# The upward products of both MLPs by seven half-size block products instead of eight

## The chip, the cores and the metric

The kernel runs on one core of a Trainium2 chip. The core has a matrix engine (PE in the profile), a vector engine (DVE), a scalar engine (ACT), a general engine (POOL) and a queue engine (SP) that issues most of the transfers (DMAs) between the chip's memory and the on-chip memory. The metric is the device time of one execution in microseconds (us); a smaller number is better.

## The reference, cut to what matters

The program is one inference step of a two-layer trunk: a Mamba-2 mixer, an MLP, an HGRN2 mixer, a second MLP and a last norm, over 512 prompt tokens and 32 sample tokens with 1024 features, all in float32. The changed part is the MLP, which stands twice:

```python
def rmsnorm(x, w):
    xf = x.astype(jnp.float32)
    y = xf * lax.rsqrt(jnp.mean(xf * xf, axis=-1, keepdims=True) + EPS)
    return (y * w.astype(jnp.float32)).astype(x.dtype)

def squared_relu_mlp(u, w_up, w_down):          # w_up (1024, 4096), w_down (4096, 1024)
    return jnp.square(jax.nn.relu(u @ w_up)) @ w_down

h = h + squared_relu_mlp(rmsnorm(h, norm_mlp_w[layer]), mlp_w_up[layer], mlp_w_down[layer])
```

## The kernel before

Features lie on the 128 partitions and the 544 tokens along the free axis, so a tile is 128 features by 544 tokens. `x` is kept as eight such tiles. A weight "unit" is 128 by 1024 words: for one tile of output features, eight blocks of 128 by 128, one for each tile of input features.

A float32 product is made of three products in a shorter format. Weight and operand are each split into a high part (`hi`, `uh`, `gh`), made by a cast on ACT, and the rest (`lo`, `ul`, `gl`), made by a subtraction on DVE; `split` does both. `products` then issues, for each of the k blocks and each half of the tokens (272 columns), hi by hi, hi by low and low by hi, so a unit takes 8 times 3 times 2 = 48 matmuls.

The weights arrive in the order of their use. `load_unit` issues one DMA of 512 KB into one of three buffers `raw`; `conv_unit` splits it into one of two pairs `whi`, `wlo`; `unit(u)` sees to it that unit u+1 is converted when unit u is used.

`mlp` runs in two halves of the 4096 inner features. In each half it makes 16 tiles of the inner layer: `up` makes the product in two banks of the accumulation memory (`pm`), DVE takes it out with relu and the factor 1/rms (`a`), ACT squares it, and `split` makes `gh`, `gl`. Then come the eight tiles of the output (`pd`), each over 16 inner tiles with two units, and `add_to_x` on DVE adds each to `x`. The accumulators `acc_tile` have two buffers of two banks; `mx` has four buffers of one bank.

The first `up` products run on the operand `uops`, that is x times the norm's weight and split, without 1/rms, since this comes later. Work that can run beside the large products is written as a generator and given to `background`; `tick` in `products` advances it by a step now and then, and `drain` runs what is left. The order in which instructions stand in each engine's queue is set by a scheduler from the program's text. `tc.high_priority()` lets the weight splits and the emptying of accumulators go ahead. Each engine runs its queue strictly in that order.

At the end of the second MLP `finish` makes the last output tile, one half of the tokens after the other, with the final norm and the output behind each.

Of the kernel before, what the change touches and what calls it, by code (L numbers as in the profile page):

```python
# [9 lines left out]
F32 = mybir.dt.float32  # L10
# [31 lines left out]
# ticks between the steps of what runs behind the large products: of the four groups of the first mixer, and of  # L42
# the pair weights and the states of the second
# [11 lines left out]
# columns of the small per-feature vectors, 128 features to a column  # L55
# [11 lines left out]
def trunk(ctx: ExitStack, tc: tile.TileContext, io):  # L67
# [31 lines left out]
    # the array's clock rises after some microseconds of work: products of zeros while the first loads are on the way  # L99
# [5 lines left out]
    ready = {}  # L105
    loaded = dict(enumerate(first))
    state = {"load": 2, "conv": 0}

    def load_unit():
        u = state["load"]  # L110
        if u >= N_UNITS:
            return
        state["load"] += 1
        raw = wraw.tile([P, 1024], F32, tag="raw", name=f"raw{u}")
        nc.sync.dma_start(raw, io["W"][u])
        loaded[u] = raw

    load_unit()
# [6 lines left out]
    def conv_unit():  # L125
        u = state["conv"]
        if u >= N_UNITS:
            return
        state["conv"] += 1
        with tc.high_priority() if u > 2 else ExitStack():  # L130
            while state["load"] <= min(u + 1, N_UNITS - 1):
                load_unit()
            raw = loaded.pop(u)
            hi = wcv.tile([P, 1024], F32R, tag="whi", name=f"whi{u}")
            lo = wcv.tile([P, 1024], F32R, tag="wlo", name=f"wlo{u}")
            for a in (0, 512) if u < 2 else (None,):
                c = slice(None) if a is None else slice(a, a + 512)
                split(raw[:, c], hi[:, c], lo[:, c], nc.gpsimd if 3 < u < U_MLP and u % 3 == 0 else None)
        ready[u] = (hi, lo)

    def unit(u):
        while state["conv"] <= min(u + 1, N_UNITS - 1):
            conv_unit()
        return ready.pop(u)
# [31 lines left out]
    def products(ps, hi, lo, ops, first, last):  # L176
        """ps[P, 2, HF] += w.T @ op over the k-tiles; hi, lo: (P, k, P); ops: k pairs of hi, lo."""
# [21 lines left out]
    def newton(ms, n):  # L199
        """ms ** -0.5 for ms > 0 of shape (p, n)."""  # L200
# [12 lines left out]
    def rstd_steps(scale, name, res, where, wait):  # L213
        """Along the free axis, the rows of 1 / rms of the tokens from their sums of squares in ssq."""
# [17 lines left out]
    def scaled_split(t, col, hi, lo):  # L232
        """hi + lo = t * col"""
# [11 lines left out]
    uh = [pers.tile([P, T], F32R, tag=f"uh{k}", name=f"uh{k}") for k in range(KT)]  # L245
    ul = [pers.tile([P, T], F32R, tag=f"ul{k}", name=f"ul{k}") for k in range(KT)]
    uops = list(zip(uh, ul))

    def pre_norm(v0):
        """For each tile of x: the operand x * w, split, and the sums of squares; 1 / rms multiplies the product."""  # L250
        def tile_done(k):
            scaled_split(x[k], vec[:, v0 + k : v0 + k + 1], uh[k], ul[k])
# [19 lines left out]
    # =====================================================================================  # L272
    def ssd(then):
# [24 lines left out]
        # x * w, split, and 1 / rms, which multiplies the products  # L298
# [25 lines left out]
        def conv_tile(u, ct, dst, rep):  # L324
            """One 128-feature tile of x, B, C: projection, causal convolution, silu."""
# [21 lines left out]
            # sample sequence s gives its four tokens at columns 515 + 7 s  # L347
# [26 lines left out]
        def silu2(u, zs, z):  # L374
            """zs = 2 silu(z)"""
# [4 lines left out]
        def first_gates():  # L380
            """The first four tiles of z: two side by side as x comes in; 1 / rms follows."""
# [26 lines left out]
        def normed():  # L408
            """The operand with 1 / rms in it."""
            for k in range(KT):  # L410
                t = pool.tile([P, T], F32, tag="st", bufs=4, name=f"xn{k}")
                if k % 3 == 1:
                    nc.gpsimd.tensor_tensor(t, x[k], rb, MUL)
                    scaled_split(t, vec[:, V_NMIX0 + k : V_NMIX0 + k + 1], uh[k], ul[k])
                else:
                    nc.vector.scalar_tensor_tensor(t, x[k], vec[:, V_NMIX0 + k : V_NMIX0 + k + 1], rb, MUL, MUL)
                    split(t, uh[k], ul[k])
# [4 lines left out]
        def scan(g, BT, CT, xs, par):  # L422
            """The recurrence of one group of 8 heads; its 4 tiles (two heads each) go to yr[g]."""
# [7 lines left out]
            def weights(c):  # L431
                """exp of the differences of the running sums, for 8 heads"""
# [7 lines left out]
            def tokens(c):  # L440
                """x * dt and x * dt * tail, tokens on partitions"""
# [13 lines left out]
            def inside(c):  # L455
                """The tokens of a chunk among themselves, and its part of the state"""
# [17 lines left out]
            def before(c):  # L474
                """What the tokens of a chunk take from the state before it"""
# [828 lines left out]
```

## Time and profile before

| | before |
|---|---|
| median of three runs | 1610.85 us (1610.6 to 1611.68) |
| span of the profiled execution, which is its own time in the trace | 1613.7 us |
| PE busy | 1572.6 us, 97% of the span |
| DVE busy | 966.1 us, 60% |
| ACT busy | 630.6 us, 39% |
| POOL busy | 145.4 us, 9% |
| granted clock of PE, mean over the span | 0.987 |
| first MLP, first `up` product to last `pd` product | 499.6 to 881.4 us |
| second MLP, the same, with its finish | 1211.4 to 1592.6 us |

The span is measured from the first to the last instruction of one profiled execution. The runs are executions of the same program without the profiler, 2.85 us below this span in the median. In the groups of the profile, a row gives line, engine, operation, output and inputs with their shapes, the count, the busy time in us and the mean duration of one in ns, then the idle time of the engine just before these instructions and what ended it. In the chain of waits a row gives start, duration and what ran.

### The profile page before, as it was taken

The numbers are of one execution on the slowest core, as the hardware profiler recorded it, in microseconds if no ns is written. First come the engines' busy times: TensorE is split into PE (matmuls) and PEld (weight loads), VectorE is DVE, ScalarE is ACT, GpSimd is POOL, SyncE is SP. The second block draws the span as 40 slices with busy tenths as digits, with TensorE's granted clock in tenths as the row PEclk, the third lists the DMA queues.
The fourth block names the chain that finished last, engine by engine and source line by source line (L and its number), as shares of the span: only waits on it lengthen the run. The fifth ranks groups of instructions, "written<-read, shape, count | busy, mean of one in ns | idle before, by whom it ended". The sixth has DMA issues, their size and how long they took to land.

```text
span 1613.7 us, 32119 instructions
## 1 busy us (share of the span) xinstructions
PE 1572.6 (97%) x13708; PEld 1515.9 (94%) x13708; DVE 966.1 (60%) x1654; ACT 630.6 (39%) x1135; POOL 145.4 (9%) x160
## 2 busy tenths in 40 slices
PE   8997989999999999999999999999999999999997
PEld 7896979989899999999999999999999999999997
DVE  7879787877876432244433688888875432244333
ACT  5485665756334431133332333333344331134321
POOL 4313131141310000000000000000000000000001
PEclk9998999999999999999999999999999999999998
DMA  5353444364232222232223222223222222322221
GB/s 182 109 156 103 160 120 157 101 197 120 88 103 85 87 92 89 82 92 92 90 89 118 70 93 91 85 91 111 81 93 80 92 81 90 92 85 86 92 92 56
DMA packets 74287, 164.38 MB, mean 102 GB/s; under 512 B 11105, under 2 KB 37761, under 8 KB 74145
## 3 DMA queue, kind: packets, MB, share of 16 engines
q1 hardware_dynamic: 72880, 161.19, 32.3%
q8 instruction: 108, 1.77, 0.5%
q10 hardware_dynamic: 1264, 1.14, 0.2%
q14 instruction: 35, 0.28, 0.1%
HBM read 145.13 MB, written 17.18 MB: 101 GB/s over the span
## 4 chain that ended last, share of the span: by engine, by line
PE 82%; DVE 5%; ACT 3%; DMA 2%; issue 2%; POOL 0%; SPq 0%; POOLq 0%; ACTq 0%; DVEq 0%
PE pm L182 24%; PE pd L182 23%; PE ps L182 18%; PE po L182 4%; PE pho L182 3%; DMA w<-cum_d 1%; PE pa L902 1%; PE py L468 1%; PE pu L459 1%; ACT w L436 1%; DVE wlo L123 1%; DVE ssq L243 1%; PE pi L484 1%; PE pn L603 1%; PE po L1028 0%
## 5 line engine op out<-in xcount | busy, mean ns | idle before, releaser
L122 ACT CAST whi<-raw 128x1024 fp32r<-128x1024 f32 (+1 forms) x226 | 235.3, 1041 | 686.1 <-PE pd L182 236.1
L123 DVE TENSOR_TENSOR wlo<-raw,whi 128x1024 fp32r<-128x1024 f32 (+1 forms) x209 | 259.7, 1242 | 164.2 <-ACT whi L122 153.0
L182 PE MATMUL ps<-uh,whi 128*128 128x272 f32 x1088 | 238.3, 300 | 1.6 <-ACT uh L122 0.8
L182 PE MATMUL ps<-ul,whi 128*128 128x272 f32 x1088 | 227.8, 291 | 0.5 <-DVE ul L123 0.5
L182 PE MATMUL ps<-uh,wlo 128*128 128x272 f32 x1088 | 228.2, 291 | 0.0
L182 PE MATMUL pm<-uh,whi 128*128 128x272 f32 x1024 | 212.0, 288 | 0.0
L182 PE MATMUL pm<-uh,wlo 128*128 128x272 f32 x1024 | 211.9, 288 | 0.0
L182 PE MATMUL pm<-ul,whi 128*128 128x272 f32 x1024 | 211.1, 288 | 0.0
L182 PE MATMUL pd<-gl,whi 128*128 128x272 f32 x992 | 204.8, 288 | 0.0
L182 PE MATMUL pd<-gh,whi 128*128 128x272 f32 x992 | 204.6, 288 | 0.0
L182 PE MATMUL pd<-gh,wlo 128*128 128x272 f32 x992 | 204.6, 288 | 0.0
L182 PEld LDWEIGHTS ps<-uh,whi 128*128 128x128 f32 x1088 | 172.8, 191 | 12.9 <-issue 6.5
L182 PEld LDWEIGHTS ps<-ul,whi 128*128 128x128 f32 x1088 | 173.5, 191 | 1.0 <-DVE ul L123 0.7
L182 PEld LDWEIGHTS ps<-uh,wlo 128*128 128x128 f32 x1088 | 172.7, 191 | 0.1
L797 DVE SCALAR_TENSOR_TENSOR a<-pm,m_rb 128x544 f32<-128x544 f32 x64 | 46.4, 725 | 195.6 <-PE pm L182 190.5
L182 PEld LDWEIGHTS pm<-uh,whi 128*128 128x128 f32 x1024 | 161.0, 188 | 0.0
L182 PEld LDWEIGHTS pm<-ul,whi 128*128 128x128 f32 x1024 | 160.9, 188 | 0.0
L182 PEld LDWEIGHTS pm<-uh,wlo 128*128 128x128 f32 x1024 | 159.9, 189 | 0.0
L182 PEld LDWEIGHTS pd<-gh,wlo 128*128 128x128 f32 x992 | 155.9, 188 | 0.0
L182 PEld LDWEIGHTS pd<-gh,whi 128*128 128x128 f32 x992 | 155.8, 188 | 0.0
L182 PEld LDWEIGHTS pd<-gl,whi 128*128 128x128 f32 x992 | 155.7, 188 | 0.0
L268 DVE TENSOR_TENSOR x<-pd,x 128x544 f32<-128x544 f32 x31 | 22.5, 725 | 122.0 <-PE pd L182 122.0
(354 smaller groups left out, 2236.2 us busy)
## 6 DMA issues: line engine op xcount, KB each, us to landing
raw<-in_W SPq DMA_DIRECT2D x222, 512.0 KB, 3.6
st<-in_ssm_in SPq DMA_DIRECT2D x16, 512.0 KB, 6.2
w<-cum_d SPq DMA_DIRECT2D x16, 512.0 KB, 5.5
out_ssm_s<-st SPq DMA_DIRECT2D x16, 512.0 KB, 3.7
hst<-in_hgrn_in SPq DMA_DIRECT2D x8, 512.0 KB, 4.3
out_hgrn_s<-hst SPq DMA_DIRECT2D x8, 512.0 KB, 4.4
E<-cum_d SPq DMA_DIRECT2D x24, 128.0 KB, 4.3
x<-in_xT SPq DMA_DIRECT2D x3, 544.0 KB, 6.7
```

Of the source, the lines that this page charges most:

```text
L122: nc.scalar.copy(hi, raw)
L123: (eng or nc.vector).tensor_tensor(lo, raw, hi.bitcast(F32), SUB)
L182: nc.tensor.matmul(ps[:, h, :HF], w[:, k, :], o[:, h * HF : (h + 1) * HF], start=(first and k == 0 and j == 0), stop=(last and k == n - 1 ...
L243: nc.vector.tensor_tensor(ssq[:, :T], ssq[:, :T], sq, ADD)
L268: nc.vector.tensor_tensor(v3(x[m]), ps[:, :, :HF], v3(x[m]), ADD)
L436: nc.scalar.activation(w[:, h], w[:, h], AF.Relu, bias=tok[:, 1, c, 8 * g + h : 8 * g + h + 1], scale=-1.0)
L459: nc.tensor.matmul(pu, bt[:, c], xts[c].rearrange("p h q -> p (h q)"), start=True, stop=True)
L468: nc.tensor.matmul(py[64 * (h % 2) : 64 * (h % 2) + 64, (h // 2) * P : (h // 2 + 1) * P], xds[c][:, h], ws_[c][:, h], start=True, stop=True,)
L484: nc.tensor.matmul(pi[:, j * P : (j + 1) * P], hT[:, j * P : (j + 1) * P], CT[:, cs], start=True, stop=True)
L603: nc.tensor.matmul(pn, bm[:, s], xq.rearrange("p h q -> p (h q)"), start=True, stop=True)
L797: nc.vector.scalar_tensor_tensor(v3(a), ps[:, :, :HF], 0.0, v3(res[0]), MAX, MUL)
L902: nc.tensor.matmul(pv4[b * NS : (b + 1) * NS, c], K[:, bs], QQ[:, 2 - n :, bs], start=True, stop=True, tile_position=(0, b * NS),)
```

## The change

Let the weights of two neighbouring tiles of inner features be a 2 by 2 arrangement of blocks: two tiles, each with its first four and its last four k blocks. The operand is cut alike: four and four tiles of input features, first and second half of the tokens. The product of the two is eight products of half size (12 matmuls each), and the change makes it from seven, by the scheme of Strassen in Winograd's form. The weight sums that it needs are made from the loaded weights, the operand sums once for each MLP, and the outputs are combined after the products.

- `MLP_GROUPS` is 4: the inner features are now in four groups of 8 tiles instead of two of 16. Each group's output products run over 8 inner tiles with one unit, so that each `x` tile is added to four times instead of twice for each MLP.
- The first group's eight tiles are made as before, 48 matmuls a tile. During its `pd` products `operands` makes the seven split operands (`b1`, two halves of `b2` and four halves of `t`) from the norm's operand. It adds high and low part on POOL, multiplies by 1/rms on DVE, and forms the sums; it does so in twelve steps, two ticks apart.
- The other three groups run in 4 pairs of tiles with the products `p1 p2 n6 q7 n5 p3 q4` (12 matmuls each, `seventh`); `SLOTS` interleaves the pairs, 7 slots a pair. `n6`, `n5` and `p3` go on in the bank of `p1`, and `q4` in that of `q7`; the values in between are copied out (`s1`, `sv`, `sw`, on ACT) and subtracted or added by DVE.
- For a pair, `load_next` loads the first tile's unit as `raw`, and three half units (`v` in two halves, and `a22`) for the second one. Then two DMAs that POOL issues add a half unit from memory onto `v` (`accum_op`). `form` makes the seven half-size weights: two sums `s2` on DVE and seven splits (`fh` on ACT, `fl` on DVE), with six buffers each. `v`, `a22` and `s2` have two buffers each.
- `_mlp_plan` writes the order out: the last output product of a group is cut in three pieces between the first products of the next, and the last two products of a group stand between pieces of the first two output products.
- `finish` now makes the last two output tiles, over 8 inner tiles each, in the same number of matmuls as before.

The function `g_tiles` squares a tile and splits it into `gh`, `gl` (ACT, ACT, DVE). The mixers' instructions stand as before on all engines.

```diff
+SLOTS = (("p1", 0), ("p2", 1), ("n6", 3), ("q7", 4), ("n5", 6), ("p3", 9), ("q4", 12))
+MLP_GROUPS = 4
+def _mlp_plan(ub):
+    plan = []
+    for q in range(MLP_GROUPS):
+        b = ub + 16 * q
+        if q == 0:
+            plan += [("u", b + i) for i in range(8)]
+        else:
+            slots = sorted((7 * i + t, name, b + 2 * i) for i in range(4) for name, t in SLOTS)
+            slots = [x[1:] for x in slots]
+            last = plan.pop()
+            piece = lambda k0, k1: last[:2] + (k0, k1) + last[4:]
+            plan += [piece(0, 4)] + slots[:2] + [piece(4, 6)] + slots[2:4] + [piece(6, 8)] + slots[4:]
+        downs = [("d", b + 8 + m, 0, 8, m, q) for m in range(KT)]
+        if q:
+            cut = lambda x, k0, k1: x[:2] + (k0, k1) + x[4:]
+            tail = plan[-2:]
+            plan[-2:] = [cut(downs[0], 0, 4), tail[0], cut(downs[0], 4, 6), tail[1], cut(downs[1], 0, 6), cut(downs[0], 6, 8), cut(downs[1], 6, 8)]
+            downs = downs[2:]
+        plan += downs
+    return plan
...
+    def load_next():
...
+            v = mp["w"].tile([P, 1024], F32, tag="v", bufs=2, name=f"v{u}")
+            a22 = mp["w"].tile([P, 512], F32, tag="a22", bufs=2, name=f"a22_{u}")
+            nc.sync.dma_start(v[:, :512], io["W"][u + 1][:, 512:])
+            nc.sync.dma_start(v[:, 512:], io["W"][u][:, :512])
+            nc.sync.dma_start(a22, io["W"][u + 1][:, 512:])
+            for c in (0, 512):
+                nc.gpsimd.dma_start(v[:, c : c + 512], io["W"][u + 1][:, :512], accum_op=ADD)
...
+    def form(name, u):
+        a1 = loaded["u", u]
+        v, a22 = loaded["v", u] if name not in ("p1", "p2") else (None, None)
+        if name == "n6":
+            s2 = mp["w"].tile([P, 512], F32, tag="s2", bufs=2, name=f"s2_{u}")
+            nc.vector.tensor_tensor(s2, v[:, 512:], a22, ADD)
+            loaded["s2", u] = s2
+        if name == "q7":
+            s2 = loaded["s2", u]
+            nc.vector.tensor_tensor(s2, s2, a1[:, 512:], ADD)
+        raw = {
+            "p1": lambda: a1[:, :512], "p2": lambda: a1[:, 512:], "n6": lambda: s2, "q7": lambda: v[:, 512:],
+            "n5": lambda: v[:, :512], "p3": lambda: loaded["s2", u], "q4": lambda: a22,
+        }[name]()
+        hi = mp["w"].tile([P, 512], F32R, tag="fh", bufs=6, name=f"fh{u}_{name}")
+        lo = mp["w"].tile([P, 512], F32R, tag="fl", bufs=6, name=f"fl{u}_{name}")
+        split(raw, hi, lo)
+        return hi, lo
...
+        def operands():
+            for k in range(4):
+                n = []
+                for j in (k, k + 4):
+                    t = pool.tile([P, T], F32, tag="a", name=f"{name}_n{j}")
+                    nc.gpsimd.tensor_tensor(t, uops[j][0].bitcast(F32), uops[j][1].bitcast(F32), ADD)
+                    nc.vector.tensor_tensor(t, t, res[0], MUL)
+                    n.append(t)
+                b11, b12, b21, b22 = n[0][:, :HF], n[0][:, HF:], n[1][:, :HF], n[1][:, HF:]
...
+                split(b11, *bo)
...
+                split(n[1], *bo)
...
+                yield 2
...
+                nc.vector.tensor_tensor(t1, b11, b12, SUB)
+                nc.vector.scalar_tensor_tensor(t2, t1, -1.0, b22, MUL, SUB)
+                nc.vector.tensor_tensor(t3, b12, b22, SUB)
+                nc.vector.tensor_tensor(t4, b21, t2, ADD)
+                yield 2
+                for i, (t, (n1, n2)) in enumerate(((t12, ("n5", "n6")), (t34, ("q7", "q4")))):
...
+                    split(t, *bo)
...
+                yield 2
...
+        def seventh(name_, u):
...
+            for k in range(4):
+                oh, ol = fops[name_, k]
+                for j, (w, o) in enumerate(((hi, oh), (hi, ol), (lo, oh))):
+                    nc.tensor.matmul(
+                        ps, w[:, k, :], o, start=(name_ in ("p1", "p2", "q7") and k == 0 and j == 0),
+                        stop=(k == 3 and j == 2), skip_group_check=name_ in ("n6", "n5", "p3", "q4"),
+                    )
+            tick()
+            keep = {"p1": "s1", "n6": "sv", "n5": "sw"}.get(name_)
+            with tc.high_priority():
+                if keep:
...
+                    nc.scalar.copy(d[keep], ps)
...
+                if name_ == "p2":
+                    nc.vector.tensor_tensor(d["p1"][:, :HF], ps, d["s1"], ADD)
+                if name_ == "n5":
+                    nc.vector.tensor_tensor(d["n6"][:, HF:], d["c"], d["sw"], SUB)
+                if name_ == "q4":
+                    nc.vector.tensor_tensor(d["n6"][:, :HF], ps, d["sv"], SUB)
+                if name_ == "p3":
+                    nc.scalar.activation(d["p1"][:, HF:], ps, AF.Relu)
+            if name_ == "p2":
+                nc.scalar.activation(d["p1"][:, :HF], d["p1"][:, :HF], AF.Relu)
+            if name_ == "p3":
+                g_tiles(u, d["p1"])
+            if name_ == "q4":
+                nc.scalar.activation(d["n6"], d["n6"], AF.Relu)
+                g_tiles(u + 1, d["n6"])
```

Two places in the queues matter below. The first is DVE during the first group of output products of the first MLP. Here `x` is the residual with the product `pd` added, `wlo` the low part of a weight unit, `m0_n` a norm's operand, `m0_b` and `m0_t` the sums' operands. Before, from the first addition on:

```order
L268 TENSOR_TENSOR x_75<-pd0_0_6624,x_75 128x544
L123 TENSOR_TENSOR wlo75_6738<-raw75_6679,whi75_6737 128x1024
L123 TENSOR_TENSOR wlo76_6792<-raw76_6735,whi76_6791 128x1024
L268 TENSOR_TENSOR x_75<-pd0_1_6734,x_75 128x544
L123 TENSOR_TENSOR wlo77_6848<-raw77_6789,whi77_6847 128x1024
```

Now, from the first addition to the second:

```order
L371 TENSOR_TENSOR x_75<-pd0_0_6147,x_75 128x544
L187 TENSOR_TENSOR wlo66_6227<-raw66_6148,whi66_6226 128x1024
L919 TENSOR_TENSOR m0_t34_0_6217<-m0_n4_6181,m0_t12_0_6216 128x272
L187 TENSOR_TENSOR m0_tl0_6255<-m0_t12_0_6216,m0_th0_6254 128x544
L187 TENSOR_TENSOR m0_b1l1_6293<-m0_n1_6286,m0_b1h1_6292 128x272
L187 TENSOR_TENSOR m0_tl4_6259<-m0_t34_0_6217,m0_th4_6258 128x544
L902 TENSOR_TENSOR m0_n5_6289<-m0_n5_6289,m0_rb_5734 128x544
L916 TENSOR_TENSOR m0_t12_1_6332<-m0_n1_6286 128x272
L918 TENSOR_TENSOR m0_t34_1_6333<-m0_n1_6286,m0_n5_6289 128x272
L917 SCALAR_TENSOR_TENSOR m0_t12_1_6332<-m0_t12_1_6332,m0_n5_6289 128x272
L187 TENSOR_TENSOR m0_b2l1_6297<-m0_n5_6289,m0_b2h1_6296 128x544
L371 TENSOR_TENSOR x_75<-pd0_1_6223,x_75 128x544
```

Before, an output product took two units, 96 matmuls, and DVE had two splits and one addition for it. Now it takes 48 matmuls, and DVE has one split, one addition and nine instructions of the operands.

The second place is the end of the second group of up products in the first MLP, where the fourth pair (units 78 and 79) ends. Before, DVE had for each tile the same three instructions:

```order
L797 SCALAR_TENSOR_TENSOR a70_6555<-pm70_6506,m0_rb_5715 128x544
L123 TENSOR_TENSOR wlo72_6565<-raw72_6500,whi72_6564 128x1024
L123 TENSOR_TENSOR gl70_6559<-a70_6555,gh70_6558 128x544
L797 SCALAR_TENSOR_TENSOR a71_6617<-pm71_6568,m0_rb_5715 128x544
L123 TENSOR_TENSOR wlo73_6628<-raw73_6562,whi73_6627 128x1024
```

Now, on DVE, with `s2_90` the sum of weights for the second pair of the next group:

```order
L187 TENSOR_TENSOR fl78_p3_7264<-s2_78_7112,fh78_p3_7263 128x512
L187 TENSOR_TENSOR fl78_q4_7268<-a22_78_7045,fh78_q4_7267 128x512
L187 TENSOR_TENSOR gl76_7191<-a76_p1_7003,gh76_7190 128x544
L216 TENSOR_TENSOR s2_90_7860<-v90_7772,a22_90_7773 128x512
L981 TENSOR_TENSOR a76_n6_7069<-pc76_7070,sv_76_7067 128x272
L979 TENSOR_TENSOR a78_n6_7214<-pc78_7215,sw_78_7259 128x272
L187 TENSOR_TENSOR gl77_7244<-a76_n6_7069,gh77_7243 128x544
```

And on ACT at the same place, where before a cast of `whi`, a square and a cast of `gh` came by turns (L122, L798, L122), now:

```order
L985 ACTIVATE a78_p1_7153<-a78_p1_7153 128x272
L938 ACTIVATE a76_p1_7003<-a76_p1_7003 128x544
L186 CAST gh76_7190<-a76_p1_7003 128x544
L973 COPY sv_78_7212<-pp78_7133 128x272
L989 ACTIVATE a76_n6_7069<-a76_n6_7069 128x544
L938 ACTIVATE a76_n6_7069<-a76_n6_7069 128x544
L973 COPY sw_78_7259<-pp78_7133 128x272
L186 CAST gh77_7243<-a76_n6_7069 128x544
```

The weight sum of the next group stands ahead of the emptying of the third pair's accumulator (`pc76`) on DVE. The relu of that result stands on ACT ahead of the copy `sw_78`, without which PE may not go on to the product `p3` of the fourth pair, in the same bank.

More of the change, by code (lines that the diff above doesn't have):

```diff
@@ L125, in conv_unit @@
     def conv_unit():
-        u = state["conv"]
-        if u >= N_UNITS:
+        if state["conv"] >= len(jobs):
             return
+        (kind, u), at = jobs[state["conv"]]
         state["conv"] += 1
         with tc.high_priority() if u > 2 else ExitStack():
[L131 to L138, printed above, removed]
@@ L139, in conv_unit @@
-        ready[u] = (hi, lo)
+            while state["load"] <= min(at + 1, len(loads) - 1):
+                if loads[state["load"]][0] == "v" and not mp:
+                    break
+                load_next()
+            if kind == "u":
+                raw = loaded.pop(("u", u))
+                hi = wcv.tile([P, 1024], F32R, tag="whi", name=f"whi{u}")
+                lo = wcv.tile([P, 1024], F32R, tag="wlo", name=f"wlo{u}")
+                for a in (0, 512) if u < 2 else (None,):
+                    c = slice(None) if a is None else slice(a, a + 512)
+                    split(raw[:, c], hi[:, c], lo[:, c], nc.gpsimd if 3 < u < U_MLP and u % 3 == 0 else None)
+            else:
+                hi, lo = form(kind, u)
@@ L141, in unit, with take @@
+    def take(key):
+        i = place[key]
+        ahead = 0.0
+        j = i
+        while j + 1 < len(jobs) and ahead < 1.0:
+            j += 1
+            ahead += 1.0 if jobs[j][0][0] == "u" else 0.25
+        while state["conv"] <= j:
+            if jobs[state["conv"]][0][0] != "u" and not mp:
+                break
+            conv_unit()
+        return ready.pop(key)
     def unit(u):
[L142 to L144 removed]
+        return take(("u", u))
```

202 lines of the change are left out of this document (135 added, 67 removed).

## The prediction

> **What bounds the kernel now.** I read the busy times first, then the chain of waits in the two MLPs, the busy times by stage, and the groups by shape of the MLP stages.
>
> ```profile
> PE 1572.6 (97%) x13708; PEld 1515.9 (94%) x13708; DVE 966.1 (60%) x1654; ACT 630.6 (39%) x1135; POOL 145.4 (9%) x160
> 505.29 87.27 PE pm L182 x696
> 592.56 96.19 PE pd L182 x768
> 688.75 96.22 PE pm L182 x768
> 784.98 96.37 PE pd L182 x768
> 1586.49 6.08 PE pd L1131 x48
> 688.00:785.00 97.00, 97.00 (x777) 97.00 (x776) 42.09 (x47) 36.06 (x47) 0.00 (x0) 1.00 0.28 88
> 592.00:688.00 96.00, 96.00 (x769) 96.00 (x768) 26.14 (x25) 18.06 (x18) 0.00 (x0) 1.00 0.28 89
> ```
>
> The chain of waits is PE alone in an MLP: 768 matmuls in 96.22 us are 125.3 ns each without a gap, at a granted clock of 1.00 (the third number from the end in a stage's row). The stages' rows give busy time of PE, weight loads, DVE, ACT and POOL. In an up stage DVE is busy for 42 of 97 us and ACT for 36; in an output stage 26 and 18 of 96. So fewer matmuls shorten the path one for one, as long as DVE and ACT, which get more to do, keep ahead. The row of L1131 has matmuls that go through one half of the tokens with another weight each time, as the new ones do: 6.08 / 48 = 126.7 ns. That the half-size products have a slower pace, so that the change doesn't do what it says, I therefore leave without a chance.
>
> **Removed from PE.** A pair of tiles takes 7 x 12 = 84 matmuls instead of 96. Twelve pairs in each MLP, two MLPs: 24 x 12 = 288 matmuls, at 125.3 ns 36.1 us. The output products and finish keep their count.
>
> **The prices of what is added.** All of it lies on DVE, ACT, POOL and the transfers. The nearest rows:
>
> ```profile
> L123 DVE TENSOR_TENSOR wlo<-raw,whi 128x1024 fp32r<-128x1024 f32 x16 | 19.6, 1225 | 1.7
> L937 DVE TENSOR_TENSOR att<-ac,bmask 128x512 f32<-128x512 f32 x8 | 5.5, 684 | 0.0
> L123 DVE TENSOR_TENSOR gl<-a,gh 128x544 fp32r<-128x544 f32 x15 | 10.9, 725 | 1.1
> L935 DVE TENSOR_TENSOR T<-f 128x272 f32<-128x272 f32 x8 | 3.5, 434 | 0.0
> L1135 DVE TENSOR_TENSOR x<-pd,x 128x272 f32<-128x272 f32 x2 | 0.9, 442 | 4.5 <-PE pd L1131 4.5
> L122 ACT CAST whi<-raw 128x1024 fp32r<-128x1024 f32 x17 | 17.8, 1049 | 64.9 <-PE pm L182 59.9 <-PE pd L182 5.0
> L122 ACT CAST whi<-raw 128x512 fp32r<-128x512 f32 x4 | 2.4, 612 | 2.2 <-DMA raw<-in_W 2.2
> L798 ACT ACTIVATE a<-a 128x544 f32<-128x544 f32 x15 | 9.9, 659 | 0.0
> L122 ACT CAST gh<-a 128x544 fp32r<-128x544 f32 x15 | 9.7, 648 | 0.5
> L334 ACT COPY pre<-ps 128x272 f32<-128x272 f32 x24 | 9.3, 388 | 0.0
> L1136 ACT ACTIVATE sq<-x 128x272 f32<-128x272 f32 x2 | 0.9, 431 | 8.1 <-DVE x L1135 8.1
> L313 POOL TENSOR_TENSOR sn_sq<-x 128x544 f32<-128x544 f32 x4 | 5.5, 1363 | 5.9 <-DMA x<-in_xT 5.9
> ```
>
> **The operands, during the first group's output products.** From the last inner tile's split to the weights of the eighth output product, DVE has 27 instructions of 544 (8 products with 1/rms, 4 low parts b2, 8 low parts t, 6 additions to x, one gl), 20 of 272, 7 weight splits and 6 instructions of 512: 27 x 0.725 + 20 x 0.434 + 7 x 1.225 + 6 x 0.684 = 41.0 us. PE needs the last of these weights after seven output products of 48 matmuls, 7 x 6.02 = 42.1 us. By that alone it fits, by one microsecond. But POOL adds high and low parts in the same stretch, six tiles of it at 1.36 us, 8.2 us, and the two engines shut each other out:
>
> ```profile
> 41.06 3.55 POOL L413 TENSOR_TENSOR xn<-x,sn_rb 128x544 f32<-128x544 f32 x1 [3.38 <-DVE ul L235]
> 42.05 1.34 DVE L123 TENSOR_TENSOR ul<-xn,uh 128x544 fp32r<-128x544 f32 x2
> 43.32 1.88 DVE L416 SCALAR_TENSOR_TENSOR xn<-x,vec,sn_rb 128x544 f32<-128x544 f32 x1
> 49.76 2.40 POOL L123 TENSOR_TENSOR wlo<-raw,whi 128x1024 fp32r<-128x1024 f32 x1 [3.12 <-ACT whi L122]
> 50.27 3.92 DVE L378 SCALAR_TENSOR_TENSOR zs<-thz,zs 128x544 f32<-128x544 f32 x3 [0.96 <-ACT thz L377]
> ```
>
> The POOL multiplication at 41.06 lasts 3.55 us, until two DVE instructions are through, and then the DVE instruction at 43.32 takes 1.88 us. Three DVE instructions of some 0.73 us that begin beside a POOL instruction at 50.27 take 3.92 us, 1.7 more. If all of it adds up, 41.0 + 8.2 - 42.1 = 7.1 us are lost in each MLP; if none, nothing. Two DVE instructions at 42.05 take 1.34 us together, less than twice 0.725, and the additions to x, which read the accumulators, may run beside POOL, so I take 3 us, nearer the lower end: 6 us for both MLPs (0 to 14). PE waits there for `wlo` of the fourth to eighth output product. [...]
>
> **The groups of pairs.** A pair now costs ACT seven casts of 512, three copies and two relus of 272, one relu, two squares and two gh of 544: 7 x 0.612 + 3 x 0.388 + 2 x 0.431 + 3 x 0.659 + 2 x 0.648 = 9.6 us. On DVE it is seven low parts and two sums of 512, three emptyings of 272 and two gl: 9 x 0.684 + 3 x 0.442 + 2 x 0.725 = 8.9 us. PE takes 84 x 0.1253 = 10.5 us for it. With the two weight units of the next output products that are split within a group of four pairs, add 0.5 us to ACT and 0.6 to DVE: 96% and 91% in the middle of a group. Over the whole group there is room, since the first pair's weights are made ahead, and an eighth output product and parts of two others lie around. In the middle the queues run late by an instruction or two. I followed three copies, behind which PE must wait to accumulate in the same bank: sv of the second pair comes about 0.5 us late (ACT waits before it for DVE, which waits for a22), sv of the fourth pair about as much, and sw of the fourth pair stands behind a chain that begins with a transfer. The two sv: 6 groups x 1.0 = 6 us (0 to 12, the upper end if each is late by a cast and a copy, 0.612 + 0.388 = 1 us).
>
> **The chain before sw.** The load of v for the next group's second pair needs the buffer that the fourth pair's n5 gives back when it is split. This split needs a buffer fl that is free after p1 of the fourth pair. From then to p3 of that pair PE has eight slots, 8 x 1.5 = 12.0 us. Within them: cast and split (0.612 + 0.684, plus some 2 us behind others in two full queues), the load, the added DMA, s2 (0.684), the emptying of q4 (0.442), relu and square (2 x 0.659), and sw (0.388). The loads:
>
> ```profile
> raw<-in_W SPq DMA_DIRECT2D x222, 512.0 KB, 3.6
> raw<-in_W SPq DMA_DIRECT2D x4, 256.0 KB, 5.4
> out_ssm_p<-hT SPq DMA_DIRECT2D x4, 256.0 KB, 2.0
> ```
>
> The load is 3.6 us. For the DMA that adds, which no row shows, the nearest are 2.0 and 5.4 us for 256 KB; I take 3.7. That makes 1.3 + 2 + 3.6 + 3.7 + 0.7 + 0.4 + 1.3 + 0.4 = 13.4 us against 12.0, 1.4 us late (none to 3.1). It happens twice in an MLP, for a third group has no next one: 4 x 1.4 = 5.6 us, 0 to 12.4. [...]
>
> **What costs nothing.** The 32 further additions to x (0.725 us) lie in output stages, where DVE has one split and one addition in 6 us. The bytes for a pair grow from 1 MB to 1.75 MB, in 10.5 us some 175 GB/s, twice the 88 to 89 of the stages' rows, with a DMA share of 0.28 there. Finish has the same matmuls, and its addition of squares runs beside the last tile's 24. If that cover were gone, it would cost two instructions, below 1 us.
>
> **The sum.** 36.1 - 6 - 6 - 5.6 = 18.5 us less: 1613.7 becomes 1595.2 us in the profiled execution, and 1610.85, the median of the runs, which lies 2.85 us below that span, becomes 1592.3.
>
> **Rivals.** *All hidden.* The queues keep ahead, since over a whole group ACT has 4 x 9.6 = 38 us to do while PE has 38 slots of 12 matmuls, 57 us (28 of the pairs, 4 of the eighth output product, 6 of two others), and the waits stay below 8 us: 1575 to 1583. [...]
>
> *ACT and DVE bound the groups.* If the new instructions take 10% longer than their nearest rows, ACT needs 10.6 + 0.5 us a pair against 10.5, and some 0.6 us is lost on three pairs of each of six groups, 11 us beyond the forecast; with the operands at their upper end another 8. That gives 1600 to 1608.
>
> *The added DMAs land late: slower.* POOL writes them out while DVE is 91% busy. If these DMAs take y us beyond 3.7, each of the four places before sw is later by y. In each of six groups the fourth pair's own s2 comes in too, once y passes some 6 us (its load goes out some nine slots before its use). Then 4y + 6(y - 6) is lost; 18.5 us are gone at y = 4.6, so it is slower from 8.3 us for an added DMA. At 10.5 us (y = 6.8) 32 us are lost: 1624. The row at 41.06 speaks for it: POOL waited 2 us there for DVE; against it, no transfer in the rows above took over 5.4 us. [...]
>
> **Chances.** The forecast (1583 to 1600) 0.44; all hidden 0.19; ACT and DVE as the bound 0.17; late DMAs 0.13, which is slower; the rest, 0.07, within 0.2% (3.2 us, about what a measurement of this kernel can tell from no change). So faster 0.80, same 0.07, slower 0.13. The range is 1575, where all is hidden, to 1612, which leaves out the late DMAs; the forecast's own range is 1583 to 1600.
>
> **What would show it.** Right: the up stages' chain of waits has 84 matmuls a pair at 125 ns; PE's idle time in an MLP is 6 to 12 us, in the first group's output products behind DVE `wlo`, and at the end of a group behind ACT `sw`. The first rival shows no such idle time, the second shows idle time before `fl` and `sv` in every pair, the third shows DVE `s2` waiting for the DMA `v`. I am wrong if PE's pace changes with the new products, or if an added DMA takes over 8 us.

## The result, and the profile after

The changed kernel took 1625.04 us in the median of four runs (1624.02 to 1626.94), the kernel before 1610.97 us beside it (1610.6 to 1611.68). The ratio is 1.0087, with a 95% interval of 1.0072 to 1.0101. The change made the kernel 14 us slower, where 18.5 us less were forecast.

The page's first rows show that the products did go away: PE has 288 matmuls less. But it is busy only 14 us less, not 36, and the span is longer, so PE must both wait and work more slowly:

```profile
span 1623.8 us, 32477 instructions
PE 1558.6 (96%) x13420; PEld 1489.0 (92%) x13420; DVE 1109.6 (68%) x1962; ACT 738.7 (45%) x1431; POOL 214.5 (13%) x224
```

From its first upward product (493.6 us before, 489.1 now) to the next mixer's first product the first MLP took 387.5 us before and takes 396.6 now; the second, to the end of its last output product, 390.0 and 394.4. (The table ahead of the change is short here: 499.6 is not the first upward product, and 1592.6 ends only the first half of the finish.) That is 13.5 us more together, near the 14.1 of the runs. With the 36.1 us that the removed matmuls were worth, about 50 us were lost in the two MLPs. The spans of the two profiles differ by only 10.1 us, because the profiled execution before came 4.5 us later to the first MLP. In the records of the runs a span lies 1.7 to 2.1 us below that run's own time, so the 2.85 us between the profile before and the median is a difference of executions.

The view of waits lists what PE waited for in the first MLP (us in total, times, longest); for the kernel before, the same view of that stretch is empty:

```profile
PE pm L282 <- DVE a L946: 3.9, 1, 3.9
PE pp L964 <- DVE a_p L977: 3.2, 2, 2.3
PE pp L964 <- ACT sw L973: 3.1, 5, 1.4
PE pd L282 <- DVE wlo L187: 2.1, 3, 1.8
PE pp L964 <- ACT s L973: 1.2, 3, 0.4
```

The first row is new to the forecast: an upward product `pm` of the *first* group, which the change left as it was, waits 3.9 us for the squared relu `a` on DVE. The chain of waits at that place (start, duration, what ran) leads from there to a transfer:

```profile
492.85 6.14 DMA v<-in_W
498.99 0.28 issue
499.27 7.03 DMA v<-in_W
506.31 0.02 issue
506.33 0.69 DVE s L216
507.02 0.65 DVE a L946
507.67 0.14 issue
507.80 4.25 PE pm L282 x20
```

L216 is `s2 = v + a22`, the first weight sum of a pair. DVE's timeline shows what it does there (in brackets the idle time before, and what ended it):

```profile
497.60 1.23 DVE L187 TENSOR_TENSOR wlo<-raw,whi 128x1024 fp32r<-128x1024 f32 x1 [0.27 <-ACT whi L186]
504.39 0.69 DVE L216 TENSOR_TENSOR s<-v,a 128x512 f32<-128x512 f32 x1 [5.56 <-DMA v<-in_W]
506.33 0.69 DVE L216 TENSOR_TENSOR s<-v,a 128x512 f32<-128x512 f32 x1 [1.25 <-DMA v<-in_W]
506.94 0.72 DVE L946 SCALAR_TENSOR_TENSOR a<-pm,m_rb 128x544 f32<-128x544 f32 x1
```

The two sums belong to pairs 72 and 74, which PE needs some 100 us later. The scheduler, to which they were given with high priority, put them in front of the squared relu that PE needs at once. DVE took them in that order, so it stood for 5.56 and 1.25 us before two loads while its next work, the squared relu, had been ready since 501.35, when ACT had copied its factor `m_rb`. What ended these waits were added DMAs, issued by POOL: the four at this place took 6.4 to 11.2 us from issue to landing. In the second MLP the first two sums stand in the same place and cost PE 3.1 us at 1233.68.

At the ends of the groups the chain before `sw` is the one that the forecast followed, with the transfers longer than it took them:

```profile
629.91 4.96 DMA a<-in_W
...
634.97 0.13 DVE s L216
...
635.58 0.45 DVE a_p L977
...
636.63 7.65 DMA v<-in_W
...
644.36 0.69 DVE s L216
645.05 0.36 DVE a_n L981
...
645.44 0.67 ACT a_n L989
...
646.13 0.66 ACT a_n L938
646.78 0.28 ACT sw L973
647.11 1.77 PE pp L964 x12
```

Here too `s2` stands on DVE in front of the emptying of a product (`a_p`, then `a_n`) and waits for `a22` and for `v`. DVE's own list of waits for the first MLP has these sums in two rows, the first with the two waits at the start in it:

```profile
DVE s L216 <- DMA v<-in_W: 17.6, 4, 5.9
DVE s L216 <- DMA a<-in_W: 8.3, 5, 2.9
```

The DMA issues give the medians from issue to landing:

```profile
v<-in_W SPq DMA_DIRECT2D x48, 256.0 KB, 4.4
v<-in_W POOLq DMA_DIRECT2D x48, 256.0 KB, 5.7
a<-in_W SPq DMA_DIRECT2D x24, 256.0 KB, 4.0
```

In the operand stage the rows by shape show DVE and POOL slowing each other. The low parts `b2l` and `b1l` were taken at 725 and 434 ns, the POOL addition at 1363:

```profile
L901 POOL TENSOR_TENSOR m_n<-uh,ul 128x544 f32<-128x544 f32 x6 | 10.1, 1677 | 27.3 <-DVE m_t L918 18.2 <-DVE m_t L919 5.9 <-ACT m_b1h L186 3.2
L902 DVE TENSOR_TENSOR m_n<-m_n,m_rb 128x544 f32<-128x544 f32 x8 | 6.9, 863 | 1.3 <-POOL m_n L901 1.3
L187 DVE TENSOR_TENSOR m_b2l<-m_n,m_b2h 128x544 fp32r<-128x544 f32 x4 | 4.9, 1215 | 0.0
L187 DVE TENSOR_TENSOR m_b1l<-m_n,m_b1h 128x272 fp32r<-128x272 f32 x4 | 4.1, 1023 | 0.0
```

And PE ran slowly for a while behind its stalls. In the chain above, 20 `pm` matmuls took 4.25 us instead of 2.5. The stages' rows (busy times of five engines, then granted clock, DMA share and GB/s) compare 3 us before that stall with 3 us behind it, behind the stall at `wlo` and behind the one at `a_p`:

```profile
500.00:503.00 3.00, 3.00 (x27) 3.00 (x26) 0.00 (x0) 0.67 (x2) 0.13 (x1) 1.00 1.08 264
508.00:511.00 3.00, 3.00 (x14) 3.00 (x15) 1.95 (x3) 2.49 (x4) 0.00 (x0) 0.50 0.00 0
572.00:575.00 3.00, 2.83 (x14) 2.84 (x15) 3.00 (x6) 2.45 (x4) 1.41 (x1) 0.60 0.54 171
636.00:639.00 3.00, 2.93 (x18) 2.94 (x18) 1.94 (x4) 2.01 (x4) 1.75 (x2) 0.74 0.35 56
```

14 matmuls instead of 27 pass in 3 us behind the first stall, at a granted clock of 0.50.

Counted by the starts of the matmuls, the delays beyond 125.3 ns for each matmul make some 50 us in the two MLPs: 18.2 us in 8 stalls above 1.2 us, 11.8 in 20 delays of 0.3 to 1.2 us, and 20.4 in 183 delays of 0.08 to 0.3 us, the slow matmuls among them. The kernel before has three delays above 0.12 us there, 1.0 us together.

### The profile page after: what moved, and what is told of

It reads as the page before. It is cut to its first block, busy times and chain, and to the rows that moved or that the text cites. A ratio compares the mean times of both kernels' runs of the same rounds, so it can differ in the third digit from the quotient of the medians.

```text
span 1623.8 us, 32477 instructions
## 1 busy us (share of the span) xinstructions
PE 1558.6 (96%) x13420; PEld 1489.0 (92%) x13420; DVE 1109.6 (68%) x1962; ACT 738.7 (45%) x1431; POOL 214.5 (13%) x224
## 4 chain that ended last, share of the span: by engine, by line
PE 72%; DVE 13%; DMA 6%; ACT 4%; issue 3%; POOL 1%; SPq 0%; POOLq 0%; DVEq 0%; ACTq 0%
PE ps L282 21%; PE pd L282 19%; PE pp L964 8%; PE pm L282 5%; PE po L282 4%; PE pc L964 3%; DMA v<-in_W 3%; PE pho L282 2%; DVE wlo L187 2%; DMA a<-in_W 2%; PE pa L1102 1%; DVE cacc L446 1%; DMA w<-cum_d 1%; ACT whi L186 1%; DVE x L371 1%
## 5 line engine op out<-in xcount | busy, mean ns | idle before, releaser
L282 PE MATMUL ps<-uh_s,whi 128*128 128x272 f32 x576 | 126.1, 300 | 1.6 <-DVE zs L501 0.8
L282 PE MATMUL ps<-ul_s,whi 128*128 128x272 f32 x576 | 121.7, 292 | 0.5 <-DVE ul_s L187 0.5
L282 PE MATMUL ps<-uh_s,wlo 128*128 128x272 f32 x576 | 121.1, 292 | 0.0
L282 PE MATMUL ps<-uh,whi 128*128 128x272 f32 x512 | 112.2, 300 | 0.0
L282 PE MATMUL ps<-uh,wlo 128*128 128x272 f32 x512 | 106.8, 288 | 0.0
L282 PE MATMUL ps<-ul,whi 128*128 128x272 f32 x512 | 106.4, 289 | 0.0
L282 PEld LDWEIGHTS ps<-ul_s,whi 128*128 128x128 f32 x576 | 92.7, 193 | 1.0 <-DVE ul_s L187 0.8
L282 PEld LDWEIGHTS ps<-uh,whi 128*128 128x128 f32 x512 | 80.6, 189 | 3.8 <-issue 1.4
L282 PEld LDWEIGHTS ps<-ul,whi 128*128 128x128 f32 x512 | 80.3, 189 | 0.0
L282 PEld LDWEIGHTS ps<-uh,wlo 128*128 128x128 f32 x512 | 80.2, 188 | 0.0
```

Of the source, the lines that this page charges most:

```text
L282: nc.tensor.matmul(ps[:, h, :HF], w[:, k, :], o[:, h * HF : (h + 1) * HF], start=(first and k == 0 and j == 0), stop=(last and k == n - 1 ...
```

## The experiments

The theory (A) was that the loss has separate parts: the sums that stand on DVE before late loads, at the starts of the MLPs and in the groups, and the operand stage, where POOL and DVE collide. The rivals were that the added DMAs cost by themselves, that the regrouping costs, or that DVE simply has too much to do. Each kernel was timed with the kernel before beside it. I compare ratios to that kernel and give their differences in us of its 1611; the changed kernel stands at +14.0. The intervals of the ratios are 1.5 to 4 us to either side.

**The sums kept in place.**

```diff
-            nc.vector.tensor_tensor(s2, v[:, 512:], a22, ADD)
+            tc.keep_in_program_order(nc.vector.tensor_tensor(s2, v[:, 512:], a22, ADD))
```

> The add `s2` (v + a22) of every pair keeps the place on DVE that the program's text gives it, behind that pair's `p2` lower half, so that it no longer stands in front of the first squared relu of each MLP. Theory A (adds that wait on DVE for late loads cost most): PE's stalls of 4.1 us and 3.2 us at the start of the MLPs go, and the slow stretch of some 1.5 us behind each, so 10 to 11 us come back: 1614 us; waits in the groups may shrink or move by 3 us either way. Rival B (the added DMAs land too late in any case): the wait only moves to the first `n6` product, and the time stays within 3 us of the changed kernel's 1625.

Measured: 1604.07 us, ratio 0.9962 (0.9946 to 0.9978), which is 6.1 us below the kernel before and 20 us below the changed kernel. That one edit turned the loss into a gain, and it was worth twice what theory A expected. DVE's timeline at the start of the first MLP has the squared relu right behind the factor that it needs, with no load before it:

```profile
496.86 1.22 DVE L187 TENSOR_TENSOR wlo<-raw,whi 128x1024 fp32r<-128x1024 f32 x1 [0.28 <-ACT whi L186]
500.63 0.73 DVE L946 SCALAR_TENSOR_TENSOR a<-pm,m_rb 128x544 f32<-128x544 f32 x1 [2.54 <-ACT m_rb L329]
```

and PE's waits in the first MLP have neither `a`, nor `a_p`, nor `sw`:

```profile
PE pd L282 <- DVE wlo L187: 3.5, 5, 1.8
PE pp L964 <- ACT s L973: 1.9, 2, 1.6
PE pp L964 <- ACT fh_n L186: 1.4, 3, 0.5
PE pp L964 <- DVE fl_n L187: 0.6, 3, 0.2
```

So the chain before `sw` went as well, and with it the term that the forecast had given it.

**Only the four sums at the MLPs' starts kept in place.**

```diff
+            add = nc.vector.tensor_tensor(s2, v[:, 512:], a22, ADD)
+            if u in (U_MLP + 16, U_MLP + 18, U_MLP2 + 16, U_MLP2 + 18):
+                tc.keep_in_program_order(add)
```

> Only the four adds that stood in front of the first squared relus (first and second pair of the second group, in each MLP) are kept in place; the twenty others keep the changed kernel's places. Theory A (two separate losses by one mechanism: 10 to 11 us at the MLPs' starts, the rest of the 21 us at the ends and middles of the later groups): 1613 to 1616. Rival I (the starts are nearly all of it): 1604 to 1608.

Measured: 1615.4 us, ratio 1.0024 (1.0012 to 1.0037), 10.1 us below the changed kernel. So the 20 us are two halves: the four sums at the starts, and the twenty later ones. DVE's later waits for `a22` are still in its list, as long as in the changed kernel; those for `v` are down from 17.6 to 5.7 us, 6.8 of it by the two at the start:

```profile
DVE s L216 <- DMA a<-in_W: 8.2, 5, 3.2
```

The two halves are not equally clean. By the order in the traces, the scheduler moved little else in this kernel, 18 of DVE's 1938 other instructions and none ahead of 600 us, so the first half belongs to the four sums. With all sums in place 78 stand elsewhere, and so do some of PE's products, all in the groups of pairs: the second half is the price of the sums' places and of what moved with them.

**The first adds of the sums on POOL.**

```diff
-            nc.vector.tensor_tensor(s2, v[:, 512:], a22, ADD)
+            nc.gpsimd.tensor_tensor(s2, v[:, 512:], a22, ADD)
```

> The first adds of the weight sums run on POOL instead of DVE, behind their DMAs in POOL's queue, so that DVE's queue never waits for `v` there; nothing else is pinned. Theory A (the harm is done by DVE standing still): as with the sums in place, 1599 to 1606. Rival J (two engines adding at once slow each other as in the operand stage, and POOL's queue now holds back the next pair's added DMAs): 1612 or more.

Measured: 1604.91 us, ratio 0.9957 (0.994 to 0.9974), the same as with the sums in place. Nothing is pinned here, and POOL makes the first two sums at 500.8 and 503.4 us, as early as DVE did in the changed kernel (504.4 and 506.3). DVE's other instructions stand nearly in the changed kernel's order, 18 of 1938 elsewhere. That it helps as much shows that the harm came from DVE's queue standing still, not from when the sums were made. Rival J falls.

**The accumulating DMAs left out, and then left out with the sums in place.** In both, `v` is its plain part alone.

```diff
-            for c in (0, 512):
-                nc.gpsimd.dma_start(v[:, c : c + 512], io["W"][u + 1][:, :512], accum_op=ADD)
```

> The accumulating DMAs are left out, so that `v` is its plain part alone; all else stays. Theory A (an accumulating DMA costs only what an add waits for it at the front of a queue): the start stalls shrink by most of their 7.3 us, the adds at the ends of the groups come 5 to 6 us earlier, in all 10 to 18 us: 1607 to 1615. Rival B (the late added DMAs are the whole loss): the full 36 us of removed products appear, about 1585 to 1592. Rival C (they cost nothing, the operands and the chain of emptying do): 1622 to 1626.

> The sums kept in place and the accumulating DMAs left out together (the weight differences are then wrong). Alone the first gave 1604.1, the second 1599.2 us. Theory A (both take away the same thing, DVE's queue standing before an add that waits for `v`): together hardly more than the second alone, 1597 to 1601, so that with the sums in place the added DMAs cost 3 to 7 us. Rival B (the DMAs cost by themselves, beside the order): the gains of 21 and 26 us add up, 1580 to 1585.

Measured: 1599.19 us, ratio 0.9933 (0.9908 to 0.9958), without the DMAs; 1603.02 us, ratio 0.9961 (0.9947 to 0.9975), without them and with the sums in place. The first missed every range: it is 24.8 us below the changed kernel, where theory A expected 10 to 18 and rival B 33 or more. The stall at the squared relu is gone although the sums still stand in front of it, since they find `v` landed. The second is the same as with the sums in place alone (0.9962). So the added DMAs cost nothing that can be measured (within some 4 us) once nothing stands in a queue before them, though with the sums in place they take about as long at the first MLP's start, 4.5 to 10.4 us; rival B, that they cost by themselves, falls. My figure for the pair, 1597 to 1601, missed. It may be that the pinned sums come a little late for `n6`: PE waited 1.4 us for `fh_n` in the first MLP with them, and not at all without them. But the two intervals overlap, and this stays open.

**The regrouping alone.** Four groups of 8 tiles, all by 48 matmuls.

```diff
-        if q == 0:
+        if True:
             plan += [("u", b + i) for i in range(8)]
```

> Only the regrouping: four groups of 8 inner tiles, all by ordinary products of 48 matmuls, no operand sums, no sevenths. Theory A: 32 more additions into x run beside the products, and the time is that of the kernel before, 1609 to 1614. Rival D (the regrouping itself costs part of what was lost): 1616 or more.

Measured: 1612.43 us, ratio 1.001 (1.0 to 1.0019), and no wait of PE in the first MLP's list. The 32 further additions to x cost at most 3 us.

**The operand sums from the high part alone.**

```diff
-                    nc.gpsimd.tensor_tensor(t, uops[j][0].bitcast(F32), uops[j][1].bitcast(F32), ADD)
-                    nc.vector.tensor_tensor(t, t, res[0], MUL)
+                    nc.vector.tensor_tensor(t, uops[j][0].bitcast(F32), res[0], MUL)
```

> The operand sums take the high part alone (the low part of the operand is left out), so that the 16 additions on POOL are gone. Theory A (DVE and POOL slow each other there, `m_b1l` took 1023 ns against 434 in my forecast): the stall of 1.92 us at `wlo` in each MLP goes with its slow stretch, 6 to 8 us in all: 1617 to 1619. Rival E (DVE's own work is too much for the stage): at most 2 us: 1623 or more.

Measured: 1617.06 us, ratio 1.0032 (1.0013 to 1.005), 8.9 us below the changed kernel. DVE does as many instructions as before, but without POOL beside it they take what the forecast's rows gave (the first number behind the bar is busy us, the second ns):

```profile
L901 DVE TENSOR_TENSOR m_n<-uh,m_rb 128x544 f32<-128x544 f32 x8 | 5.7, 715 | 0.0
L187 DVE TENSOR_TENSOR m_b2l<-m_n,m_b2h 128x544 fp32r<-128x544 f32 x4 | 2.9, 713 | 0.0
L187 DVE TENSOR_TENSOR m_b1l<-m_n,m_b1h 128x272 fp32r<-128x272 f32 x4 | 1.7, 430 | 0.0
```

Against the rows after the change, DVE saves 1.2 + 2.0 + 2.4 = 5.6 us in this stage of the first MLP, and rival E falls: it is the work beside POOL, not DVE's own amount. That POOL's result is no longer waited for plays little part: in the changed kernel DVE waited for it once in this MLP, 1.3 us.

**The operands made earlier and without POOL**, on top of the sums in place.

```diff
-                    nc.gpsimd.tensor_tensor(t, uops[j][0].bitcast(F32), uops[j][1].bitcast(F32), ADD)
-                    nc.vector.tensor_tensor(t, t, res[0], MUL)
+                nc.vector.scalar_tensor_tensor(t, x[k], vec[:, v0 + k : v0 + k + 1], res[0], MUL, MUL)
...
+                        background(norm_steps(), name + "n", wait=2)
```

> The sums kept in place (as in the first experiment), and the operand work moved: the normed operand is made on DVE alone from x, weight and 1/rms and its `b1`, `b2` are split beside the first group's upward products; only the `t` sums and splits stay beside its output products; POOL adds nothing. Theory A (the operand stage loses 3 to 4 us in each MLP to late weight splits): the stalls of 1.92, 0.79, 0.98 and 1.42, 0.76, 0.99 us at `wlo`, 6.9 us in all, go for the most part: 1597 to 1600 against 1604.1 without it. Rival E (DVE's work is only moved, and the upward products then stall): 1603 or more.

Measured: 1597.39 us, ratio 0.9916 (0.9895 to 0.9938), 7.4 us below the sums in place alone. In the first MLP no `pd` product of the first group waits any more.

**The sevenths' weights split five steps ahead instead of four**, on top of the sums in place.

```diff
-            ahead += 1.0 if jobs[j][0][0] == "u" else 0.25
+            ahead += 1.0 if jobs[j][0][0] == "u" else 0.2
```

> The sums kept in place, and the sevenths' weights split five steps ahead instead of four. Theory A (what is left in the groups is mostly the `n6` halves that come late, 0.62 and 0.37 us six times): 3 to 6 us less than 1604.1, so 1598 to 1601. Rival G (what is left is the turn of a bank behind its copy on ACT, or the earlier adds wait for `v` again): 1603 or more.

Measured: 1600.58 us, ratio 0.9941 (0.9924 to 0.9958), 3.4 us less. The interval overlaps that of the sums in place alone, so the size isn't settled and rival G isn't excluded by the time. But PE's waits for `fh_n` and `fl_n` in the first MLP, 1.4 and 0.6 us, are gone from its list.

**All three, and the same with the adds on POOL.**

> The three edits that won something, together: sums in place (-21 us from the changed kernel), operands made earlier and without POOL (6.7 us more), the split five steps ahead (3.5 us more). Theory A (three separate losses): the gains add up, 1592 to 1596. Rival H (the last two take away one and the same wait on DVE): 1597 or more.

> The sums' first adds on POOL together with the earlier operands and the split five steps ahead. Theory A (DVE then waits for no load and PE loses only the turns of the banks): no slower than the three edits with the adds on DVE, 1590 to 1596. Rival J (POOL beside DVE costs DVE time): 1598 or more.

Measured: 1592.9 us, ratio 0.9885 (0.987 to 0.99), 18.5 us below the kernel before and 32.5 below the changed kernel. The gains add up, as theory A said. With the adds on POOL 1597.77 us, ratio 0.9911 (0.9896 to 0.9926): slower than theory A allowed, so with the waits gone POOL's additions seem to cost some 4 us, though the intervals overlap. In the kernel with all three, PE's waits in the first MLP are down to

```profile
PE pp L967 <- ACT s L976: 1.3, 3, 0.6
PE pd L282 <- DVE wlo L187: 0.3, 2, 0.2
```

Of the 36.1 us, 17.6 are still not had. By the starts of the matmuls in the trace, most of them go in small steps: 18 times PE turns to a product in a bank that ACT has just copied (`s`) and starts up to 0.8 us late, 6.2 us in all; 18 times it waits for an emptying on DVE (`a_p`), 0.1 us each, 2.4 us; and the matmul after such a turn comes another 0.1 us late. That makes 2.3 to 2.6 us in each of the six groups. No experiment took these apart.

**PE's pace after an idle stretch.** The kernel before, with waits of seven lengths put in.

```diff
+                    nc.scalar.copy(v3(t[0]), old[0][:, :, :HF])
+                    for i in range(waits[u] - 1):
+                        nc.scalar.copy(t[(i + 1) % 2], t[i % 2])
...
+                    late.enter_context(tc.issue_after(nc.tensor.matmul(mx(f"wait_{u}")[:, :1], w[:, :P], w[:, :1], start=True, stop=True).ins))
```

> The kernel before, with seven waits put into the first half's upward products of each MLP: before every second tile's product one small matmul waits for a chain of 1, 2, ... 7 copies on ACT behind the last product, so that PE idles for about 0.9, 1.6, 2.2, 2.9, 3.5, 4.2 and 4.8 us. Theory A (after an idle stretch of some 2 us or more PE runs for about 3.5 us at 0.2265 us a matmul): the time grows by the idle stretches, some 40 us, and by 1.4 to 1.7 us behind each of the longer ones, 12 to 17 us: 1663 to 1668. Rival F (the slow stretches in the changed kernel had another cause, such as the operands or the banks): by the idle stretches alone, about 1650, and no stretch of slow matmuls.

Measured: 1706.26 us (one run), 96.5 us more than the kernel before beside it. PE's list of waits holds the idle time:

```profile
PE wait L802 <- ACT wait L800: 57.4, 12, 6.5
PE wait L802 <- ACT wait L798: 4.0, 2, 2.0
```

The stretches were longer than planned, 61.4 us, which is why both figures missed. Of the other 35 us, 26 are slow matmuls of the products, by their starts 1.4 to 2.6 us behind each of the fourteen waits; the small matmuls that were put in, two records for each wait, take 5.8 us. Nothing of the operands or the groups stands in this kernel, so rival F falls. The stages' rows ahead of, behind and some 4 us after the shortest of the second MLP's waits, which ended at 1277.21:

```profile
1262.00:1275.00 13.00, 13.00 (x107) 12.99 (x105) 5.74 (x10) 5.25 (x8) 0.00 (x0) 1.00 0.28 82
1277.00:1281.00 4.00, 3.79 (x18) 3.79 (x19) 1.03 (x2) 0.71 (x2) 0.00 (x0) 0.57 0.44 131
1281.00:1288.00 7.00, 7.00 (x59) 7.00 (x58) 2.51 (x3) 2.32 (x3) 0.00 (x0) 1.00 0.00 0
```

## Why the prediction was wrong, step by step

- **Removed from PE**, 36.1 us: right. 13708 matmuls became 13420, and their pace between the stalls stayed at 125 ns.
- **Costs nothing**: right for the 32 additions to x, by the regrouping alone (1.6 us, with 0 to 3). The further bytes of the pairs were not tried by themselves.
- **The operands**, 6 us in a range of 0 to 14: right in its cause, DVE and POOL slowing each other, and nearly in size. Taking POOL out of the stage gave 8.9 us, and 7.4 where the work was also moved. PE waited where it was said, at `wlo`: 1.8 us at most in each MLP, and the slow matmuls behind that wait came on top. The durations of `b1l` and `b2l` show it: 1023 and 1215 ns with POOL's additions, 430 and 713 without. That additions to x can run beside POOL, which helped to choose the 3 us an MLP, no run shows: only one in each MLP met a POOL addition, with the last 0.49 us of its 0.72, and an `m_tl` that met one for as long took no more than 0.72 either. Why less than the 14 us of the upper end was lost, no run shows.
- **The chain before `sw`**, 5.6 us: right in its links, too small in its size. The added DMA was taken at 3.7 us; the median was 5.7, and 7.65 in the chain shown. A second place was missing, `a_p` behind a sum that waits for `a22`, up to 2.3 us of waiting. The twenty sums of the groups, with what moved when they were pinned, were worth 10.0 us. And the chain ran through the sum only because the sum stood on DVE ahead of the emptying; with the sums in place it was not there.
- **The step that failed** is the count in this chain, "It happens twice in an MLP". The forecast saw that a sum of the next group can stand on DVE in front of urgent work, but it looked for that only at the ends of groups of pairs, and gave the first group's upward products, which the change left as they were, no term at all. There the sums of pairs 72 and 74 stand in front of the first squared relu; DVE's timeline shows them, and I did not look for them there. These four sums, two in each MLP, were worth 10.1 us. With the 10.0 in the groups that is most of the 32.5 us between the changed kernel and the best of the experiments.
- **The rivals**: the third, late DMAs, named the row that would show it, DVE `s2` waiting for the DMA `v`, and came out at 1624, next to the measured time. That is half luck. Four added DMAs did take over 8 us, the sign that was named, but all of them at the starts of the MLPs (up to 11.2 us), where the rival has no term; at the places that it priced they took 3.8 to 7.8 us, not over 8.3. And they cost only through the sums' places in the queue. POOL's instruction for each lasted 0.85 to 1.55 us; that DVE's work held up the writing of them, for which the forecast had only the row at 41.06, no run shows. The second, ACT and DVE as the bound, is seen in part: `fh_n`, `fl_n` and the copies `s` came late, worth perhaps 3.4 us. Its two terms and the forecast's two `sv` (6 us) can't be told apart by the runs. Its range also doesn't follow from its terms: 11 and 19 us beyond 1592.3 give 1603 to 1611, not 1600 to 1608.
- **What was not in the sum at all**: the turns of the banks, of which the forecast followed only `sv` and `sw` (some 14 us in the best kernel), and the slow matmuls after a stall. Behind the stalls of 4.1, 1.9, 2.5, 3.2 and 1.9 us (507.80, 572.16, 636.07, 1233.68, 1298.05) some 13 to 16 matmuls ran at half the pace, 1.4 to 1.6 us more each time, some 7.5 us of the 50.

The best kernel's 1592.9 us lies close to the forecast of 1592.3. That is no confirmation: its loss of 17.6 us is as large as the three terms together, but the operand term and the chain before `sw` were removed from it, and the turns of the banks took their place.

## What to carry to other kernels

Here a sum that waited for a transfer held up all that stood behind it in DVE's queue, for 5.56 us, though its own result was wanted some 100 us later. When a change adds such an instruction with a priority, look up where the scheduler put it and what follows it there, above all far ahead of its use; giving it a place behind work of its own time, or to an engine with nothing urgent behind it, took 20 us off here. A stall of PE of 2.5 us and more was followed here by another 1.4 to 2.6 us of slow matmuls; one of 2 us by as much or by nothing.

## What the runs showed of the hardware that I had not expected

PE's granted clock fell to 0.50 behind five short stalls in the changed kernel's MLPs, and stayed there for 3.41 us each time (from 507.72, 572.57, 637.43, 1234.76 and 1299.61); in the next 2.8 to 3 us it was 1.00 again. I counted a stall as the time between the starts of two matmuls less 125 ns. All 18 stalls of 2.48 us and more that I found in the MLPs of the traces were followed by 13 to 25 matmuls at 0.2265 us instead of 0.1253. Of 18 stalls between 1.9 and 2.4 us, 8 were and 10 were not; of 14 stalls of 1.4 to 1.85 us one was followed by 18, the others by at most a few. The same wait at `wlo` shows both. In the changed kernel PE's idle time there was 1.75 us, the clock behind it 0.60; with the sums in place it was 1.76 us, and 23 matmuls passed in the next 3 us at 1.00:

```profile
565.70:568.70 3.00, 2.97 (x23) 2.97 (x24) 3.00 (x5) 2.58 (x4) 1.54 (x1) 1.00 0.52 175
```
